# Sixty-four tokens of a product-key expert layer leave the dense grid for gathered rows on VectorE

## The chip, the cores and the metric

The kernel runs as one program on one core of one Trainium2 chip. The metric is the time of one execution in microseconds of device time. Engines are named as in the profile: PE is TensorE (PEld its weight loads), DVE is VectorE, ACT is ScalarE, POOL is GpSimd, SP the queue that issues most DMAs. Each engine runs its instructions in its own fixed order; an instruction waits until its inputs are there and its buffer is free, and all that is behind it on its engine waits with it.

## The reference

One layer of a decoder for 256 tokens of width 2048, float32: a mixer (sliding-window attention and an mLSTM, gated and merged), and then a channel mixer that looks experts up. The change touches only the second.

```python
qp = (xt @ w_peer_q).reshape(T, 8, 2, 128)
scores = einsum('thcd,hcnd->thcn', qp, peer_keys)        # 128 keys in each half
s_top, i_top = top_k(scores, 16)
cand = s_top[:, :, 0, :, None] + s_top[:, :, 1, None, :]
top_s, pos = top_k(cand.reshape(T, 8, 256), 16)
idx = take_along_axis(cand_idx, pos)                     # 16 of 16384 experts per head
gates = softmax(top_s)
act = gelu(einsum('td,thkd->thk', xt, peer_u[idx]))
x = x + einsum('thk,thkd->td', gates * act, peer_v[idx])
```

So each token has 8 x 16 = 128 experts of its own among 16384; each expert has one row of u and one of v, 2048 numbers (8 KB) each.

## The kernel before

All 256 tokens are worked against all 16384 experts. The experts lie in 128 blocks of 128. In the stage **u** TensorE makes, for each block, the products of 128 experts with 256 tokens; ScalarE takes the Gelu of them into a big table W (parts wA and wB, experts on the partitions, tokens along a row). The 128 gates of a token are *scattered* into that table: a one-hot matrix A (first index) and B (second index) are built for four tokens at a time and multiplied on TensorE (line 853), and the product with the table leaves zero everywhere but at the token's own experts. In the stage **v** TensorE multiplies the table with all of v into eight banks of PSUM that stay open through the stage.

Matmuls run in the type float32r, and each float32 operand is split into a rounded part `hi` (a ScalarE copy, line 84) and the rest `lo` (a VectorE subtraction, line 85). A product is made of three parts: hi·hi, hi·lo and lo·hi.

All weights stream in *units* of 128x1024 (512 KB): `load` has four buffers (raw), hi and lo have two each. Function `run` walks through a list of units; for each it issues the load and the split of the next unit, then the matmuls of the present one, and then as many entries of a list of small tasks (`side`: the top-16 searches, the lookups, the scatters) as the rate in its call allows. A u unit is half a block (`ws_units`): eight 512-column matmuls (line 158: X holds the hi and lo of 256 tokens side by side) and eight of 256 columns (line 162). A v unit has twelve 512-column matmuls (lines 889 to 893), with the table's column as the weights.

The work is written as such a program order, and the instructions of each engine are then put into a fixed order by the framework's scheduler, which moves an instruction forward where it thinks that its engine would be free. So the order on an engine isn't always that of the code. The rates in the code are hints to it.

Stages after the mixer: w_o with the residual x1, the query projection (w_pq, 32 units, with `score` and `top16`), u in two calls of `run` (52 blocks with the rest of the searches, `pick16`, `lookup` and `turn`; then 76 blocks with the scatters), v, and the output. The tile X (64 KB a partition) holds the tokens' operand and later the residual.

Of the kernel before, what the change touches and what calls it, by code (L numbers as in the profile page):

```python
# [29 lines left out]
LOW = -3.0e38  # L30
HU = 1024
QU = 512


@with_exitstack
def hybrid_block_kernel(ctx: ExitStack, tc: tile.TileContext, a, out):
# [10 lines left out]
    def pool(stack, name, bufs=1):  # L47
        return stack.enter_context(tc.tile_pool(name=name, bufs=bufs, reuse_waits="tile"))
# [34 lines left out]
    def split(hi, lo, src):  # L83
        S.activation(hi, src, AF.Copy)  # L84
        V.tensor_sub(lo, src, hi.bitcast(F32))  # L85
# [45 lines left out]

# [704 lines left out]
    W[1] = wpool.tile([P, NE - NA, T], F32, name="wB")  # L836
    TG = 4
    NAB = 8

    def scatter(t0):  # L840

        AB = []
        for j in range(TG):
            t = t0 + j
            AB.append(eb.tile([P, 2, NK], F32, name="ab", bufs=NAB))
            A, B = AB[j][:, 0], AB[j][:, 1]
            S.activation(B, iot, AF.Square, bias=i1T[:, t:t + 1])  # L847
            S.activation(B, B, AF.Relu, bias=1.0, scale=-1.0)
            V.tensor_scalar(A, iot, i0T[:, t:t + 1], gT[:, t:t + 1], op0=OP.is_equal, op1=OP.mult)  # L849
        yield  # L850
        ps = psd.tile([P, TG, NK], F32, name="sd")
        for j in range(TG):
            PE.matmul(ps[:, j], AB[j][:, 1], AB[j][:, 0], start=True, stop=True)  # L853
        yield
        m = done["e"]
        for s, (lo, hi) in enumerate(((0, NA), (NA, NE))):
            for x0, x1, mul in ((lo, min(max(m, lo), hi), True), (max(min(m, hi), lo), hi, False)):
                if x1 <= x0:
                    continue
                dst = W[s][:, x0 - lo:x1 - lo, t0:t0 + TG].rearrange("p i t -> p t i")  # L860
# [4 lines left out]
        done["tok"] = t0 + TG  # L865
# [6 lines left out]
    acc = [[(psd, pmm)[t].tile([P, QU], F32, name=("sd", "mm")[t]) for q in range(4)] for t in range(NT)]  # L872
    pw = {}
    x1 = xx.tile([P, NT, D], F32, name="X")
    nc.sync.dma_start(x1, x1d.rearrange("(t p) d -> p t d", p=P))

    def v_consume(i, h):
        def f(parts):
            if h == 0:
                ph = eb.tile([P, T], F32R, name="ph", tag="ab", bufs=NAB)  # L880
                pl = eb.tile([P, T], F32R, name="pl", tag="ab", bufs=NAB)
                split(ph, pl, wv(i))
                pw[i] = (ph, pl)
            ph, pl = pw[i]
            hi, lo = [[part[:, q * QU:(q + 1) * QU] for q in range(HU // QU)] for part in parts]
            todo = [(q, t) for q in range(HU // QU) for t in range(NT)]
            for q, t in todo:
                ts = slice(t * P, (t + 1) * P)
                PE.matmul(acc[t][h * 2 + q], ph[:, ts], hi[q], start=(i == 0), stop=False)  # L889
                PE.matmul(acc[t][h * 2 + q], pl[:, ts], hi[q], start=False, stop=False)  # L890
            for q, t in todo:
                ts = slice(t * P, (t + 1) * P)
                PE.matmul(acc[t][h * 2 + q], ph[:, ts], lo[q], start=False, stop=(i == NE - 1))  # L893
        return f

    units = []
    for i in range(NE):
        for h in range(2):
            units.append((a["v"][i * P:(i + 1) * P, h * HU:(h + 1) * HU], v_consume(i, h)))
    run(units)  # L900
    for q in range(4):
        for t in range(NT):
            o = x1[:, t, q * QU:(q + 1) * QU]
            V.tensor_add(o, acc[t][q], o)
            nc.sync.dma_start(out[t * P:(t + 1) * P, q * QU:(q + 1) * QU], o)


# [59 lines left out]
```

## Time and profile before

| | |
|---|---|
| time, median of 3 runs | 2269.59 us (2269.19 to 2269.6) |
| the profiled execution | 2268.72 us, span of the trace 2267.0 us |
| busy in the span | PE 99%, PEld 84%, DVE 71%, ACT 55%, POOL 4% |
| moved | 415.66 MB, 183 GB/s on average |
| TensorE's granted clock | full (0.999 on average) |

The span runs from the first instruction to the last; the execution's time has a little around it. A matmul's recorded length reaches from its issue to its modelled end and overlaps the next one's, so its price is the distance between starts. The profile's stretches used below, in us from the start of the span: 684 to 778 the query projection, 778 to 1067 the first 52 blocks of u, 1067 to 1556 the other 76, 1556 to 2262 v.

### The profile page before, as it was taken

The page shows a single profiled execution, that of the slowest core. Times are in us where ns is not written, and L with a number is a line of the kernel's source. Part 1 is how long each engine was busy: PE and PEld are TensorE (multiplying, and loading weights), DVE is VectorE, ACT ScalarE, POOL GpSimd, SP SyncE. Part 2 cuts the span into 40 slices and gives each one's busy share as a digit, 9 for nine tenths or more (in the row PEclk, how much of TensorE's full clock was granted, in tenths as well). Part 3 has the DMA queues.
Part 4 walks back from the last instruction along what each step waited for, and adds up shares of the span by engine and source line. Part 5 has one row for each costly group of instructions (what it writes and reads, how often), then busy time and mean ns, then how long its engine had stood idle before and what let it go on. Part 6 is the DMA issues. An engine that isn't in the chain of part 4 may idle for free.

```text
span 2267.0 us, 32407 instructions
## 1 busy us (share of the span) xinstructions
PE 2235.2 (99%) x11841; PEld 1906.3 (84%) x11841; DVE 1599.0 (71%) x2915; ACT 1257.8 (55%) x2378; POOL 85.9 (4%) x79
## 2 busy tenths in 40 slices
PE   7999999999999999999999999999999999999999
PEld 5887788888888878888888888888888888888887
DVE  7977688778889997855777788886555555555555
ACT  5755566556544444544777777775444444444443
POOL 3000000000130020200000000000000000000000
PEclk9999999999999999999999999999999999999999
DMA  6565544555665445555544444556555555555555
GB/s 204 189 191 164 169 160 160 184 186 189 211 212 188 162 164 196 181 190 186 171 165 166 165 163 167 165 170 213 195 195 193 193 194 193 194 194 193 194 192 173
DMA packets 115296, 415.66 MB, mean 183 GB/s; under 512 B 12992, under 2 KB 13120, under 8 KB 114752
## 3 DMA queue, kind: packets, MB, share of 16 engines
q1 hardware_dynamic: 115136, 413.59, 55.1%
q8 instruction: 92, 1.51, 0.3%
q14 instruction: 68, 0.56, 0.1%
HBM read 409.35 MB, written 4.19 MB: 182 GB/s over the span
## 4 chain that ended last, share of the span: by engine, by line
PE 91%; DVE 7%; ACT 1%; POOL 1%; issue 0%; DMA 0%; POOLq 0%; SPq 0%; DVEq 0%
PE mm L158 33%; PE mm L162 17%; PE sd L890 5%; PE sd L889 5%; PE mm L889 5%; PE mm L890 5%; PE sd L893 5%; PE mm L893 5%; PE sd L853 3%; DVE lo L85 2%; PE mm L184 2%; PE mm L185 2%; PE mm L189 2%; DVE oh L805 0%; DVE xg L257 0%
## 5 line engine op out<-in xcount | busy, mean ns | idle before, releaser
L85 DVE TENSOR_TENSOR lo<-raw,hi 128x1024 fp32r<-128x1024 f32 x762 | 936.5, 1229 | 611.3 <-ACT hi L84 603.4
L84 ACT ACTIVATE hi<-raw 128x1024 fp32r<-128x1024 f32 x762 | 807.0, 1059 | 863.1 <-PE mm L890 378.5
L158 PE MATMUL mm<-X,hi 128*128 128x512 f32 x3088 | 789.8, 397 | 13.8 <-ACT hi L84 8.5
L158 PEld LDWEIGHTS mm<-X,hi 128*128 128x128 f32 x3088 | 557.4, 190 | 117.7 <-ACT hi L84 8.8
L162 PEld LDWEIGHTS mm<-X,lo 128*128 128x128 f32 x3088 | 421.1, 190 | 39.7 <-DVE lo L85 9.7
L162 PE MATMUL mm<-X,lo 128*128 128x256 f32 x3088 | 433.6, 283 | 5.0 <-DVE lo L85 5.0
L889 PE MATMUL sd<-hi,ph 128*128 128x512 f32 x512 | 199.2, 389 | 0.0
L890 PE MATMUL sd<-hi,pl 128*128 128x512 f32 x512 | 199.2, 389 | 0.0
L890 PE MATMUL mm<-hi,pl 128*128 128x512 f32 x512 | 199.2, 389 | 0.0
L889 PE MATMUL mm<-hi,ph 128*128 128x512 f32 x512 | 199.2, 389 | 0.0
L893 PE MATMUL sd<-lo,ph 128*128 128x512 f32 x512 | 199.2, 389 | 0.0
L893 PE MATMUL mm<-lo,ph 128*128 128x512 f32 x512 | 199.2, 389 | 0.0
L889 PEld LDWEIGHTS mm<-hi,ph 128*128 128x128 f32 x512 | 96.1, 188 | 20.1
L893 PEld LDWEIGHTS sd<-lo,ph 128*128 128x128 f32 x512 | 96.1, 188 | 20.0
L890 PEld LDWEIGHTS mm<-hi,pl 128*128 128x128 f32 x512 | 96.1, 188 | 19.9
L889 PEld LDWEIGHTS sd<-hi,ph 128*128 128x128 f32 x512 | 96.1, 188 | 19.9
L893 PEld LDWEIGHTS mm<-lo,ph 128*128 128x128 f32 x512 | 96.1, 188 | 19.9
L890 PEld LDWEIGHTS sd<-hi,pl 128*128 128x128 f32 x512 | 96.0, 188 | 19.9
L184 PE MATMUL mm<-hi,X 128*128 128x512 f32 x224 | 89.6, 400 | 0.0
L847 ACT ACTIVATE ab<-iot,i1T 128x128 f32<-128x128 f32 x256 | 87.8, 390 | 1.4 <-DVE i1T L823 1.4
L185 PE MATMUL mm<-hi,X 128*128 128x512 f32 x224 | 88.2, 394 | 0.0
L849 DVE TENSOR_SCALAR ab<-iot,i0T,gT 128x128 f32<-128x128 f32 x256 | 74.2, 345 | 0.0
(279 smaller groups left out, 2082.4 us busy)
## 6 DMA issues: line engine op xcount, KB each, us to landing
raw<-u SPq DMA_DIRECT2D x256, 512.0 KB, 3.7
raw<-v SPq DMA_DIRECT2D x256, 512.0 KB, 3.6
raw<-w_g SPq DMA_DIRECT2D x64, 512.0 KB, 3.6
raw<-w_tok SPq DMA_DIRECT2D x56, 512.0 KB, 3.6
raw<-w_qk SPq DMA_DIRECT2D x32, 512.0 KB, 3.7
raw<-w_o SPq DMA_DIRECT2D x32, 512.0 KB, 4.0
raw<-w_pq SPq DMA_DIRECT2D x32, 512.0 KB, 3.7
raw<-w_pa SPq DMA_DIRECT2D x16, 512.0 KB, 3.5
```

Of the source, the lines that this page charges most:

```text
L84: S.activation(hi, src, AF.Copy)
L85: V.tensor_sub(lo, src, hi.bitcast(F32))
L158: PE.matmul(ps, hi[:, w], X[:, k].rearrange("p s t -> p (s t)"), start=(k == 0), stop=False)
L162: PE.matmul(ps[:, :T], lo[:, w], X[:, k, 0], start=False, stop=(k == kts - 1))
L184: PE.matmul(st["ps"][t], xh[:, k, ts], hi[q], start=(k == 0), stop=False)
L185: PE.matmul(st["ps"][t], xl[:, k, ts], hi[q], start=False, stop=False)
L847: S.activation(B, iot, AF.Square, bias=i1T[:, t:t + 1])
L849: V.tensor_scalar(A, iot, i0T[:, t:t + 1], gT[:, t:t + 1], op0=OP.is_equal, op1=OP.mult)
L853: PE.matmul(ps[:, j], AB[j][:, 1], AB[j][:, 0], start=True, stop=True)
L889: PE.matmul(acc[t][h * 2 + q], ph[:, ts], hi[q], start=(i == 0), stop=False)
L890: PE.matmul(acc[t][h * 2 + q], pl[:, ts], hi[q], start=False, stop=False)
L893: PE.matmul(acc[t][h * 2 + q], ph[:, ts], lo[q], start=False, stop=(i == NE - 1))
```

## The change

Tokens 0 to 63 leave the table. For them the rows of their own experts are gathered from memory: `fetch` is an indirect DMA on POOL's queue that brings 128 half rows of 1024 numbers (4 KB), one to a partition: partitions 0 to 63 hold the first half of the row for the 64 tokens, 64 to 127 the second. One fetch serves one of the 128 expert slots, so there are 128 fetches from u and 128 from v, 512 KB each, into six slabs in the place of the tile X. `dot` multiplies a slab with the tokens and sums along the row on VectorE; `own_weights` adds the two halves on TensorE, takes the Gelu and the gate; `add_row` adds a v row times its weight into `xs_`.

The other 192 tokens (ND) stay on TensorE, now already scaled with the norm: `xg` is written to memory while w_o runs, read back and split into Xn. A u unit has 24 matmuls of 192 columns, three for each weight block of 128x128, and ends in PSUM without a sum or scaling by VectorE; a v unit has 24 as well, with the blocks of v as the weights and the table's column (in the ring in Xn's place) moving, so that the output comes out transposed and is turned back in `finish`. The scatter runs for 192 tokens, with the one-hot A for four tokens in one VectorE instruction and the gate moved into ScalarE's Relu. The second token tile's top-16 searches are put behind the first's lookups.

```diff
+SP = 64
+ND = T - SP
+HD = D // 2
@@ step
+        if rows_todo:
+            pace[1] += row_rate[0]
+            if pace[1] >= 1.0:
+                pace[1] -= 1.0
+                rows_todo.pop(0)()
@@ evac_out
+            S.dma_start(xgd[:, n], xg[:, SP:])
@@
-    NA = 80
-    wA = exc.tile([P, NA, T], F32, name="wA")
+    Xn = exc.tile([P, KT, 2, ND], F32R, name="Xn")
+    NA = 74
+    wA = exc.tile([P, NA, ND], F32, name="wA")
+    def load_xg():
+        nc.sync.dma_start(wA[:, 0:KT], xgd)
+    def norm_xg(c):
+        xs = wA[:, 4 * c:4 * c + 4]
+        V.tensor_mul(xs, xs, rb[:, SP:].unsqueeze(1).to_broadcast([P, 4, ND]))
+        split(Xn[:, 4 * c:4 * c + 4, 0], Xn[:, 4 * c:4 * c + 4, 1], xs)
+    side += [load_xg] + [lambda c=c: norm_xg(c) for c in range(KT // 4)]
@@ u_units
-            z = eb.tile([P, T], F32, name="zu")
-            total(z, ps)
-            V.tensor_mul(z, z, rb)
-            later.append(lambda: act_u(i, z))
+                for j in range(per):
+                    k = h * per + j
+                    w = slice(j * P, (j + 1) * P)
+                    PE.matmul(o, hi[:, w], Xn[:, k, 0], start=(k == 0), stop=False)
+                    PE.matmul(o, hi[:, w], Xn[:, k, 1], start=False, stop=False)
+                for j in range(per):
+                    k = h * per + j
+                    w = slice(j * P, (j + 1) * P)
+                    PE.matmul(o, lo[:, w], Xn[:, k, 0], start=False, stop=(k == KT - 1))
+                if h == KT // per - 1:
+                    later.append(lambda: act_u(i, ps))
-    E0 = 52
+    E0 = 44
@@ the rows of tokens 0 to 63
+    sp = xx.tile([P, 2 * KT * T], F32, name="X")
+    NSL = 6
+    slab = [sp[:, j * HD:(j + 1) * HD] for j in range(NSL)]
+    def fetch(table, s):
+        G.indirect_dma_start(out=slab[s % NSL], out_offset=None, in_=tables[table],
+                             in_offset=bass.IndirectOffsetOnAxis(ap=ix[:, s:s + 1], axis=0))
+    def own_rows():
+        V.tensor_scalar(ixf, ixf, 2.0, half, op0=OP.mult, op1=OP.add)
+        V.tensor_copy(ix, ixf)
+        for s in range(NSL):
+            fetch("u", s)
+        rows_todo.extend([lambda s=s: dot(s) for s in range(NS)])
+    def dot(s):
+        V.scalar_tensor_tensor(slab[s % NSL], slab[s % NSL], 1.0, xs_, op0=OP.mult, op1=OP.mult,
+                               accum_out=dots[:, s:s + 1])
+        if s + NSL < NS:
+            fetch("u", s + NSL)
+    def add_row(s):
...
+            V.scalar_tensor_tensor(xs_, slab[s % NSL], wgt[:, s:s + 1], xs_, op0=OP.mult, op1=OP.add)
+        if s + NSL < NS:
+            fetch("v", s + NSL)
@@ calls
-    run(u_units(0, E0), 0.75)
+        if t == 0:
+            side += [own_index, lambda: None, lambda: None, lambda: None, own_rows]
+    own_x()
+    row_rate[0] = 0.7
+    run(u_units(0, E0), 1.0)
@@ scatter
+        V.tensor_tensor(A, iot.unsqueeze(1).to_broadcast([P, TG, NK]),
+                        i0T[:, t0:t0 + TG].unsqueeze(2).to_broadcast([P, TG, NK]), op=OP.is_equal)
-    side += [scatter(t0) for t0 in range(0, T, TG)]
+    side += [scatter(t0) for t0 in range(SP, T, TG)]
@@ v
-                PE.matmul(acc[t][h * 2 + q], ph[:, ts], hi[q], start=(i == 0), stop=False)
-                PE.matmul(acc[t][h * 2 + q], pl[:, ts], hi[q], start=False, stop=False)
+            for o, b, w in blocks:
+                PE.matmul(o, hi[:, w], ph, start=False, stop=False)
+                PE.matmul(o, hi[:, w], pl, start=False, stop=False)
+            for o, b, w in blocks:
+                PE.matmul(o, lo[:, w], ph, start=False, stop=(i == NE - 1 and b % 2 == 1))
+    rows_todo += [lambda s=s: add_row(s) for s in range(NS)]
+    row_rate[0] = (NS + 1) / (len(units) - 2 * LAST - 2)
```

The engines' orders, first VectorE's in the u stage. Line 85 before and line 88 now is the lo split of a unit; 199 and 769 are the sum and scaling of a u block, 805 and 808 a lookup. Before, in the first part of u:

```order
L85 TENSOR_TENSOR lo<-raw,hi 128x1024
L199 TENSOR_TENSOR zu<-mm,zu 128x256
L808 TENSOR_REDUCE iv<-oh 128x16
L769 TENSOR_TENSOR zu<-zu,rb 128x256
L808 TENSOR_REDUCE iv<-oh 128x16 x2
L85 TENSOR_TENSOR lo<-raw,hi 128x1024
```

And now, from the tenth unit of u on (912 is a dot, 848 the lookup's first instruction):

```order
L844 CAST abf<-ab 128x256
L912 SCALAR_TENSOR_TENSOR X<-X 128x1024
L848 TENSOR_TENSOR oh<-abf,a_7748 128x256 x2
L912 SCALAR_TENSOR_TENSOR X<-X 128x1024
L848 TENSOR_TENSOR oh<-abf,a_7748 128x256
L912 SCALAR_TENSOR_TENSOR X<-X 128x1024 x2
L88 TENSOR_TENSOR lo<-raw,hi 128x1024
L912 SCALAR_TENSOR_TENSOR X<-X 128x1024 x6
L88 TENSOR_TENSOR lo<-raw,hi 128x1024
```

The sum and scaling are gone. All 128 dots stand between the sixth lo split of u and the thirty-third, five or six in most of these 27 gaps; after the last of them some forty gaps hold a lo split and nothing else. The code's rate was 0.7 dots a unit.

VectorE in the v stage: `pl` before and the split into Xn now is the split of the table's column, 936 the weighted add of a row. Before, all through v:

```order
L85 TENSOR_TENSOR pl<-wA,ph 128x256
L85 TENSOR_TENSOR lo<-raw,hi 128x1024 x2
L85 TENSOR_TENSOR pl<-wA,ph 128x256
L85 TENSOR_TENSOR lo<-raw,hi 128x1024 x2
L85 TENSOR_TENSOR pl<-wA,ph 128x256
```

Now, from the sixth unit of v on:

```order
L936 SCALAR_TENSOR_TENSOR X<-X 128x1024 x6
L88 TENSOR_TENSOR lo<-raw,hi 128x1024
L88 TENSOR_TENSOR Xn<-wA,Xn 128x192
L936 SCALAR_TENSOR_TENSOR X<-X 128x1024 x5
L88 TENSOR_TENSOR lo<-raw,hi 128x1024
L936 SCALAR_TENSOR_TENSOR X<-X 128x1024 x5
```

The 128 adds stand in the first 25 gaps of v, up to the twenty-sixth lo split, though the code spreads them over 242 units.

TensorE at the change from the query projection to u. Before (730 is `score`):

```order
L162 MATMUL mm<-X,lo 128x256 x6
L730 MATMUL sd<-keysT,zu 128x128 x2
L162 MATMUL mm<-X,lo 128x256 x2
L158 MATMUL mm<-X,hi 128x512 x8
L162 MATMUL mm<-X,lo 128x256 x8
```

Now, at the end of u's first unit (the pair of 811 and 812 stands eight times before the eight of 816):

```order
L811 MATMUL mm<-Xn,hi 128x192
L812 MATMUL mm<-Xn,hi 128x192
L816 MATMUL mm<-Xn,lo 128x192 x8
L811 MATMUL mm<-Xn,hi 128x192
L812 MATMUL mm<-Xn,hi 128x192
```

A unit had 16 matmuls and has 24, of 192 columns each; the scatters and transposes keep their places between units.

## Rows read from the trace of the kernel before

**Rows 1.** The page: engines' busy time and share; the chain that ended last.
```profile
PE 2235.2 (99%) x11841; PEld 1906.3 (84%) x11841; DVE 1599.0 (71%) x2915; ACT 1257.8 (55%) x2378; POOL 85.9 (4%) x79
...
PE 91%; DVE 7%; ACT 1%; POOL 1%; issue 0%; DMA 0%; POOLq 0%; SPq 0%; DVEq 0%
```

**Rows 2.** Windows: stretch, length, busy PE PEld DVE ACT POOL, clock, DMA share, GB/s.
```profile
684.00:778.00 94.00, 92.14 (x527) 79.12 (x528) 89.36 (x339) 41.48 (x61) 0.00 (x0) 1.00 0.50 171
778.00:1067.00 289.00, 283.47 (x1614) 245.81 (x1613) 218.15 (x420) 146.12 (x223) 36.51 (x32) 1.00 0.55 182
1067.00:1556.00 489.00, 489.00 (x2985) 436.62 (x2984) 381.66 (x738) 357.03 (x969) 0.00 (x0) 1.00 0.50 167
1556.00:2262.00 706.00, 705.59 (x3128) 584.48 (x3126) 364.15 (x396) 313.00 (x387) 0.00 (x0) 1.00 0.59 194
```

**Rows 3.** Timeline of TensorE in a scatter unit: start, length (us), line.
```profile
1199.73 1.12 PE L162 MATMUL mm<-X,lo 128*128 128x256 f32 x8
1200.68 1.06 PE L853 MATMUL sd<-ab 128*128 128x128 f32 x8
```

**Rows 4.** Windows, a stretch of v.
```profile
1700.00:1800.00 100.00, 100.00 (x443) 82.81 (x442) 50.75 (x56) 45.05 (x56) 0.00 (x0) 1.00 0.58 192
```

**Rows 5.** Groups by shape: busy us, mean ns, idle; 128-column passes, loads of weights.
```profile
L853 PE MATMUL sd<-ab 128*128 128x128 f32 x512 | 66.3, 275 | 0.0
...
L853 PEld LDWEIGHTS sd<-ab 128*128 128x128 f32 x512 | 62.1, 192 | 0.0
...
L518 PEld LDWEIGHTS sd<-pT,av 128*64 128x64 f32 x48 | 2.4, 134 | 3.9 <-issue 3.7 <-ACT hi L84 0.2
```

**Rows 6.** Timeline of TensorE, plain f32 matmuls of 257 columns, two passes each.
```profile
332.07 0.59 PE L574 MATMUL sd<-v,dT 128*128 128x257 f32 x2
332.50 0.60 PE L575 MATMUL sd<-v,dT 128*128 128x257 f32 x2
```

**Rows 7.** Groups by shape, VectorE.
```profile
L85 DVE TENSOR_TENSOR lo<-raw,hi 128x1024 fp32r<-128x1024 f32 x762 | 936.5, 1229 | 611.3 <-ACT hi L84 603.4 <-PE sd L853 4.5 <-ACT sr L78 0.6
...
L85 DVE TENSOR_TENSOR pl<-wA,ph 128x256 fp32r<-128x256 f32 x80 | 33.4, 419 | 0.2 <-ACT ph L84 0.2
...
L85 DVE TENSOR_TENSOR X<-xg,X 128x256 fp32r<-128x256 f32 x32 | 23.8, 765 | 0.6 <-ACT X L84 0.6
...
L356 DVE SCALAR_TENSOR_TENSOR ac<-zqk,acol,ac 128x256 f32<-128x256 f32 x48 | 23.2, 483 | 0.6
...
L805 DVE TENSOR_TENSOR oh<-abf,a 128x256 f32<-128x256 f32 x32 | 14.2, 481 | 0.0
...
L808 DVE TENSOR_REDUCE iv<-oh 128x16 f32<-128x256 f32 x32 | 12.7, 411 | 4.9 <-POOL oh L807 4.9
```

**Rows 8.** DMA queue (page), start of the kernel (windows), landing of loads (DMA issues).
```profile
q1 hardware_dynamic: 115136, 413.59, 55.1%
...
10.00:15.00 5.00, 1.90 (x5) 1.54 (x6) 5.00 (x14) 3.08 (x7) 3.11 (x5) 1.00 1.03 416
...
raw<-u SPq DMA_DIRECT2D x256, 512.0 KB, 3.7
```

**Rows 9.** Groups by shape, GpSimd.
```profile
L807 POOL TENSOR_TENSOR oh<-oh,itf 128x256 f32<-128x256 f32 x32 | 36.5, 1159 | 224.1 <-DVE gs L815 119.2 <-DVE oh L805 104.9
...
L684 POOL TENSOR_TENSOR sqa<-sqa,sq 128x256 f32<-128x256 f32 x15 | 26.5, 1767 | 60.7 <-ACT sq L680 60.7
...
L249 POOL TENSOR_TENSOR sq<-xt 128x256 f32<-128x256 f32 x5 | 3.2, 643 | 0.1
```

**Rows 10.** Groups by shape, ScalarE.
```profile
L84 ACT ACTIVATE hi<-raw 128x1024 fp32r<-128x1024 f32 x762 | 807.0, 1059 | 863.1 <-PE mm L890 378.5 <-PE mm L158 277.4 <-issue 126.9
...
L847 ACT ACTIVATE ab<-iot,i1T 128x128 f32<-128x128 f32 x256 | 87.8, 390 | 1.4 <-DVE i1T L823 1.4
...
L848 ACT ACTIVATE ab<-ab 128x128 f32<-128x128 f32 x256 | 64.5, 299 | 0.1
```

**Rows 11.** Timelines of TensorE and VectorE at the end.
```profile
2261.20 0.39 PE L893 MATMUL mm<-lo,ph 128*128 128x512 f32 x1
...
2262.75 0.68 DVE L904 TENSOR_TENSOR X<-mm,X 128x512 f32<-128x512 f32 x1
```

More of the change, by code (lines that the diff above doesn't have):

```diff
@@ L97, in parts_of @@
         return hi, lo
-    side, later = [], []
-    pace = [0.0]
+    side, later, rows_todo = [], [], []
+    pace = [0.0, 0.0]
+    row_rate = [0.0]
     def tick():
@@ L732, in score @@
         for t in range(NT):
-            side.append(lambda t=t: top16(sc[:, t, n], st_[:, t, n], it_[:, t, n]))
+            (side, second)[t].append(lambda t=t: top16(sc[:, t, n], st_[:, t, n], it_[:, t, n]))
     def evac_q(n):
@@ L745, in hybrid_block_kernel @@
         units += ws_units(a["w_pq"][n], X2, evac_q(n))
-    run(units, 0.75)
+    run(units, 0.85)
     flush()
@@ L824, in turn @@
         V.tensor_copy(gT[:, t * P:(t + 1) * P], pi[:, 2 * P:3 * P])
+        V.tensor_scalar(ngT[:, t * P:(t + 1) * P], pi[:, 2 * P:3 * P], -1.0, None, op0=OP.mult)
+    sp = xx.tile([P, 2 * KT * T], F32, name="X")
+    NSL = 6
+    slab = [sp[:, j * HD:(j + 1) * HD] for j in range(NSL)]
+    xs_ = sp[:, NSL * HD:(NSL + 1) * HD]
+    s0 = (NSL + 1) * HD
+    ixf, dots, wgt, wt = (sp[:, s0 + j * NS:s0 + (j + 1) * NS] for j in range(4))
+    ix = sp[:, s0 + 4 * NS:s0 + 5 * NS].bitcast(U32)
+    zt = sp[:, s0 + 5 * NS:s0 + 5 * NS + SP]
@@ new lines, in own_index @@
+    def own_index():
+        V.tensor_mul(xs_, xs_, slab[NSL - 1])
+        ef = tk.tile([SP, NS], F32, name="ef")
+        V.scalar_tensor_tensor(ef, iv[0:SP, 0], float(NK), iv[0:SP, 1], op0=OP.mult, op1=OP.add)
+        G.dma_start(exd, ef)
+        for c in range(2):
+            G.dma_start(ixf[c * SP:(c + 1) * SP], exd)
+    def own_rows():
[4 more added lines that the diff above has]
+        rows_todo.extend([lambda s=s: dot(s) for s in range(NS)])
@@ new lines, in dot, with own_weights @@
+    def dot(s):
[3 more added lines that the diff above has]
+            fetch("u", s + NSL)
+    def own_weights():
+        for s in range(NSL):
+            fetch("v", s)
+        zp = psd.tile([P, QU], F32, name="sd")
+        PE.matmul(zp[:, 0:SP], dots, pair, start=True, stop=True)
+        yield
+        V.tensor_mul(zt, zp[:, 0:SP], rb[:, 0:SP])
+        S.activation(zt, zt, AF.Gelu)
+        V.tensor_mul(wt.rearrange("p (c t) -> p c t", c=2), zt.unsqueeze(1).to_broadcast([P, 2, SP]),
+                     gT[:, 0:SP].unsqueeze(1).to_broadcast([P, 2, SP]))
+        yield
+        wp = psd.tile([P, QU], F32, name="sd")
+        PE.transpose(wp[:, 0:NS], wt, ident)
+        V.tensor_copy(wgt, wp[:, 0:NS])
@@ L864, in scatter @@
                     S.activation(dst, ps[:, :, x0:x1], AF.Copy)
-        done["tok"] = t0 + TG
-    side += [scatter(t0) for t0 in range(0, T, TG)]
+        done["tok"] = c0 + TG
+    side += [scatter(t0) for t0 in range(SP, T, TG)]
     run(u_units(E0, NE), 3 * len(side) / (2 * (NE - E0) - 5))
     drain()
[L872 to L875, printed above, removed]
+    while rows_todo:
+        rows_todo.pop(0)()
@@ new lines, in hybrid_block_kernel, with load_x1 @@
+    NB2 = D // P
+    acc = [(psd, pmm)[q % 2].tile([P, QU], F32, name=("sd", "mm")[q % 2]) for q in range(NB2 // 2)]
+    NR = 16
+    ring = exc.tile([P, NR, 2, ND], F32R, name="Xn")
+    zero = ring[:, NR - 1].rearrange("p s t -> p (s t)")
+    V.memset(zero.bitcast(F32), 0.0)
+    flat = wA.rearrange("p i t -> p (i t)")
+    x1 = flat[:, 0:2 * D].rearrange("p (t d) -> p t d", d=D)
+    x1s = flat[:, 2 * D:2 * D + HD]
+    def load_x1():
+        nc.sync.dma_start(x1[0:P - SP, 0], x1d[SP:P])
+        nc.sync.dma_start(x1[:, 1], x1d[P:T])
+        for c in range(2):
+            nc.sync.dma_start(x1s[c * SP:(c + 1) * SP], x1d[0:SP, c * HD:(c + 1) * HD])
@@ L877, in v_consume @@
     def v_consume(i, h):
         def f(parts):
+            ph, pl = ring[:, i % NR, 0], ring[:, i % NR, 1]
             if h == 0:
-                ph = eb.tile([P, T], F32R, name="ph", tag="ab", bufs=NAB)
-                pl = eb.tile([P, T], F32R, name="pl", tag="ab", bufs=NAB)
                 split(ph, pl, wv(i))
[L883 to L886, printed above, removed]
@@ L900, in hybrid_block_kernel @@
-    run(units)
[L901 to L905, printed above, removed]
+            hi, lo = parts
+            blocks = [(acc[b // 2][:, (b % 2) * ND:(b % 2 + 1) * ND], b, slice(j * P, (j + 1) * P))
+                      for j, b in enumerate(range(h * (NB2 // 2), (h + 1) * (NB2 // 2)))]
+            if i == 0:
+                for o, b, w in blocks[::2]:
+                    PE.matmul(acc[b // 2][:, 0:2 * ND], hi[:, w], zero, start=True, stop=False)
@@ new lines, in f, with unit, finish @@
+            for o, b, w in blocks:
[3 more added lines that the diff above has]
+                PE.matmul(o, lo[:, w], ph, start=False, stop=(i == NE - 1 and b % 2 == 1))
+        return f
+    def unit(i, h):
+        return (a["v"][i * P:(i + 1) * P, h * HU:(h + 1) * HU], v_consume(i, h))
+    def finish(q):
+        tT = slab[q][:, 0:4 * ND].rearrange("p (b t) -> p b t", t=ND)
+        S.activation(tT[:, 0:2], acc[2 * q][:, 0:2 * ND].rearrange("p (b t) -> p b t", t=ND), AF.Copy)
+        V.tensor_copy(tT[:, 2:4], acc[2 * q + 1][:, 0:2 * ND].rearrange("p (b t) -> p b t", t=ND))
+        for t in range(NT):
+            n = P - SP if t == 0 else P
+            pt = (psd, pmm)[t].tile([P, QU], F32, name=("sd", "mm")[t])
+            for b in range(4):
+                src = tT[:, b, 0:n] if t == 0 else tT[:, b, P - SP:]
+                PE.transpose(pt[0:n, b * P:(b + 1) * P], src, ident)
+            o = x1[0:n, t, q * QU:(q + 1) * QU]
+            V.tensor_add(o, pt[0:n], o)
+            nc.sync.dma_start(out[SP:P, q * QU:(q + 1) * QU] if t == 0 else out[P:T, q * QU:(q + 1) * QU], o)
@@ new lines, in own_out @@
+    def own_out():
+        V.tensor_add(xs_, xs_, x1s)
+        for c in range(2):
+            nc.sync.dma_start(out[0:SP, c * HD:(c + 1) * HD], xs_[c * SP:(c + 1) * SP])
+    LAST = 6
+    units = [unit(i, h) for i in range(NE - LAST) for h in range(2)]
+    units += [unit(i, h) for h in range(2) for i in range(NE - LAST, NE)]
+    ow = own_weights()
+    next(ow), next(ow), next(ow, None)
+    rows_todo += [lambda s=s: add_row(s) for s in range(NS)]
+    rows_todo.append(own_out)
+    row_rate[0] = (NS + 1) / (len(units) - 2 * LAST - 2)
@@ L908, with at_end, f, with_x1 @@
+    pace[1] = 0.0
+    def at_end(u):
+        def f(parts):
+            u[1](parts)
+            later.extend([lambda: finish(0), lambda: finish(1)])
+        return (u[0], f)
+    units[-LAST - 1] = at_end(units[-LAST - 1])
+    x0 = units[100]
+    def with_x1(parts):
+        x0[1](parts)
+        load_x1()
+    units[100] = (x0[0], with_x1)
+    run(units)
+    flush()
+    while rows_todo:
+        rows_todo.pop(0)()
+    finish(2)
+    finish(3)
 def kernel(**inputs):
```

78 lines of the change are left out of this document (48 added, 30 removed).

## The prediction

> **What bounds the kernel now.** I read the chain that ended last first: TensorE is 91% of it [rows 1]. Then busy time by stage [rows 2]. The four stretches are the query projection of the retrieval (684 to 778 us), the first 52 blocks of u (to 1067), the other 76 with the scatter of the gates beside them (to 1556), and v. TensorE's clock is granted in full in all of them (the 2.4 GHz level), and TensorE is busy for all but 8 us of 1578. VectorE is at 95%, 75%, 78% and 52% of its time in them, ScalarE at 44 to 73%, the DMA engines at 50 to 59%. So TensorE sets the pace, and what counts is the time from one matmul to the next, not its recorded length (matmuls overlap). The eight 256-column matmuls of a u unit take 1200.68 - 1199.73 = 0.95 us, 0.119 each [rows 3]. The 512-column ones of v: 443 in 100 us, 0.226 each [rows 4]. The eight 128-column passes of a scatter take 1.06 us in all, the last 0.275 by its own record, so (1.06 - 0.275)/7 = 0.112 each [rows 3, 5].
>
> **TensorE's part of the change.** A 128x128 block of u costs one 512-column and one 256-column matmul, 0.345 us; v costs 24 matmuls of 0.226 per expert block. The new code has three matmuls of 192 columns for a weight block in both stages, each with its own weight load, as every matmul of the trace has one [rows 1]: 2048 x 3 x 2 = 12288 matmuls, against 4096 + 3072. No row has a matmul of this type under 256 columns. From below: if the time went with the columns, 0.226 x 192/512 = 0.085. From above, two prices: 0.119, if 192 columns cost what 256 do; and 0.321, if the type lost its rate, since plain f32 passes of 257 columns stand 0.43 apart per two passes [rows 6], 1.67 ns a column. I take 0.112, the nearest row in length and the one with the same weight load: 0.192 us recorded for 128 columns of weights, 0.134 for 64 [rows 5], that is 0.9 ns a column and 0.116 for 128, so a weight load alone seems to fill what a 192-column stream leaves free. The Trainium skill (TensorE: Matmul & The Clock Gate, "LDWEIGHTS (loading the stationary operand)") says that a load lasts its columns divided by 1.2 ns, 107 ns here, whatever streams beside it. That rule speaks against this change, and by it the final sum would come to 2559 us.
>
> At 0.112: 12288 x 0.112 = 1376 us against 2048 x 0.345 + 3072 x 0.226 = 707 + 694 = 1401: 25 saved. Only 48 of 64 scatter groups stay, 16 x 8 x 0.112 = 14 saved. The eight zeroing matmuls add 1. **Sum -38 us**: three narrow matmuls are hardly cheaper than two wide ones. A unit (half a block) then takes 24 x 0.112 = 2.69 us.
>
> **VectorE's part, which decides.** What VectorE loses (the 0.42 us sum and scaling of each u block) lay beside TensorE: worth nothing. What it gains is 128 dots and 128 weighted adds on 128x1024. The nearest rows are the same operation on 256 elements, 0.483 us, and two-input work of 256 and 1024 elements, 0.419 and 1.229 [rows 7]: 0.483 + 0.810 = 1.29 us each, 165 us a stage. Spread evenly over the stages that would fit. But the order of VectorE's instructions doesn't spread them: in u all 128 dots stand in 27 gaps between one lo split and the next (from the sixth unit on, five or six to a gap), in v all 128 adds in 25 gaps. VectorE works in that order, and TensorE can run only two units ahead of the last lo (two buffers of hi and lo).
>
> In those 27 gaps of u VectorE has 165 + 27 x 1.23 = 198, and 21 of picks and lookups for the second token tile [rows 7]: 219 us, where TensorE needs 27 x 2.69 = 73. In the 25 gaps of v: 165 + 31 + 10 for 29 splits of the gates (0.35 each), 206 us against 67.
>
> The rows must arrive too: 128 gathers of 0.524 MB plus the stage's own loads, 155 x 0.524 = 81 MB in u and 80 + 2 in v. The DMA queue moved 413.59 MB in 55.1% of 2267 us [rows 8], 331 GB/s at full share, which makes 246 us; at the 416 GB/s of the start [rows 8] it is 195. So VectorE and the DMA engines need about the same time, six gathers are in flight, and they won't mesh perfectly: I take 240 us for u, 235 for v. What issuing a gather costs on GpSimd no row shows: from below nothing (hidden), from above the whole 3.7 us landing of a 512 KB load [rows 8] for one gather after another, 474 us a stage. The nearest row, GpSimd's work on 128x256, is 1.16 us [rows 9]; that is under the 1.29 of a dot, so I price it at nothing beyond the 240.
>
> TensorE's stalls: u **240 - 73 = +167**; v **235 - 67 = +168**.
>
> Smaller terms. In the four gaps before the dots, VectorE has 29 us (sixteen lookups of 0.481 + 0.411 among them), GpSimd's 16 x 1.16 in one go adds 4, and the expert numbers' way through DRAM (two landings, less 4 of other work) 2: 35 - 4 x 2.69 = 24, of which the run-up hides little: **+23**. In the query projection the reload, scaling and split of xg put 10.2 us into one gap; the others have about 2.4 against 2.77: **+5** (0 to 12). A scatter group's four Squares and four Relus (4 x 0.689, [rows 10]) stand in one ScalarE gap between hi splits, often with the next group's in the gap after it: about 8 us with the splits (1.06 each) and a Gelu, against 5.4. There are 24 such pairs; TensorE's scatter passes and hi's head start of half a unit hide most: **+10** (0 to 60). At the start of v the gate splits reuse the place of Xn and must wait for u's last matmul, then the weights of the rows go matmul, product, Gelu, product, transpose, copy: **+6** (3 to 12). At the end two last transposed quarters replace four adds; now 5.8 us lie between the last matmul's start and the end of the span [rows 11]: **+4**. The early place of the row output among SP's loads (after 30 of 256) costs nothing, since VectorE finishes those adds at the same place.
>
> **Sum**, on the profiled execution's 2268.7 us (span 2267.0; 0.9 under the median): 2268.7 - 38 + 5 + 23 + 167 + 10 + 6 + 168 + 4 = 2614. The saving on TensorE is real and small; two stretches in which everything waits for gathered rows cost nine times as much. Behind them what is late next is TensorE again, at 2.69 us a unit.
>
> **Rivals.**
> (a) *Gather and dot hold each other up.* GpSimd's adds took 1.77 us beside a busy VectorE, its products 0.64 in a calmer place [rows 9], and VectorE's split of X beside those adds 0.765 on average, against 0.419 for the same shape elsewhere [rows 7]: +0.35, up to 0.55 in the worst. If a gather costs GpSimd 1.77 and lengthens a dot by 0.55, one after the other, a gather's period is 2.3: 128 x 2.3 + 33 = 327 in u, 335 in v. That adds 87 + 100: 2801 us. Against it: six slabs let issue and dot overlap. The Trainium skill (SBUF — State Buffer, "Who interferes with whom") says that a VectorE instruction with two SBUF inputs contends with a GpSimd instruction that reads SBUF; the split's row agrees, and dots and adds have two such inputs.
> (b) *The narrow matmul loses its rate*: 0.321 us. For it: plain f32 does run so [rows 6]. Against it: one weight load and one pass stand for each such matmul, as for the wide ones. Then 12288 x (0.321 - 0.112) = 2568 more, a unit of 7.7 us covers the row work (the three stalls go, -358): 4824 us.
> (c) *Faster, the other side: the time goes with the columns*, weight loads hidden. For it: from 256 to 512 columns the price rises by 0.107, nearly in proportion. Against it: 128-column passes cost 0.112. The stalls stay, since VectorE sets them, and TensorE's cheaper units make them longer. With the gathers hidden too (219 and 206) the total is 1328 + 11040 x price (12288 matmuls, less 52 x 24 inside the two stretches): at 0.085, 2266 us, no slower than before. It decides at 0.0852 us.
> (d) *The row work doesn't stall anything*, because VectorE's idle time (25% and 48% of u and v) takes it: 2614 - 358 = 2256. Only with the dots spread over the stage; the order has them in 27 and 25 gaps.
>
> **How the numbers follow.** Forecast 62%, (a) 18%, (b) 10%, (c) 3%, (d) 2%; 5% for something slower that I haven't named. The likeliest case's own range is 2490 to 2710: low with VectorE alone as the limit (219, 206: -50), no ScalarE or projection loss (-15) and the matmul at 0.107 (11040 x 0.005 = -55); high with 0.119 (+77) and more of ScalarE's clumps. To hold 8 in 10 the range must take in (a); the upper bound of gathers one after another is 2614 + 234 + 239 = 3087. I give 2470 to 3000. (b), (c) and (d) are left out, with 15%, and a little at either end. About 0.2% (4.5 us) is what a measurement can tell from no change: (d) and half of (c) make faster 3%, the other half and a little of (d) same 2%, and the rest slower, 95%.
>
> **What would show it.** In u's first 33 units and v's first 26 TensorE should be busy a third of its time, VectorE near full, DMA share over 0.9, and the span of each stretch near 240 us. The dots should last 1.29. Outside them matmuls should start 0.112 apart and a unit take 2.7 us, TensorE full. If VectorE shows idle time before the dots and ends it on a DMA, and GpSimd's issue is longer than 1.3 us, (a) holds. If matmuls of 192 columns stand 0.3 us apart, (b). I am wrong altogether if VectorE's trace has the dots spread over the stage, or lo splits passing them.

## The result: 2599 us against 2269

The changed kernel took 2599.23 us (median of 4 runs, 2595.2 to 2601.38), the kernel before 2269.39 (4 runs): a ratio of 1.1452, 95% interval 1.1432 to 1.1472. Forecast were 2614, in 2470 to 3000. The profiled execution has a span of 2598.9 us, 331.9 longer.

### The profile page after: what moved, and what is told of

It reads as the page before. It is cut to its first block, busy times and chain, and to the rows that moved or that the text cites. A ratio compares the mean times of both kernels' runs of the same rounds, so it can differ in the third digit from the quotient of the medians.

```text
span 2598.9 us, 42839 instructions
## 1 busy us (share of the span) xinstructions
PE 2335.0 (90%) x16876; PEld 2200.9 (85%) x16876; DVE 1771.0 (68%) x2843; ACT 1205.0 (46%) x2113; POOL 421.1 (16%) x343
## 5 line engine op out<-in xcount | busy, mean ns | idle before, releaser
L811 PE MATMUL mm<-Xn,hi 128*128 128x192 f32 x2048 | 516.7, 291 | 6.8 <-ACT hi L87 6.3
L812 PE MATMUL mm<-Xn,hi 128*128 128x192 f32 x2048 | 511.2, 289 | 0.0
L811 PEld LDWEIGHTS mm<-Xn,hi 128*128 128x128 f32 x2048 | 425.0, 208 | 9.8 <-ACT hi L87 9.8
L812 PEld LDWEIGHTS mm<-Xn,hi 128*128 128x128 f32 x2048 | 424.6, 207 | 0.0
L816 PE MATMUL mm<-Xn,lo 128*128 128x192 f32 x2048 | 300.3, 293 | 131.3 <-DVE lo L88 131.3
L816 PEld LDWEIGHTS mm<-Xn,lo 128*128 128x128 f32 x2048 | 274.4, 208 | 138.1 <-DVE lo L88 138.1
L1025 PE MATMUL sd<-Xn,lo 128*128 128x192 f32 x1024 | 212.6, 290 | 90.1 <-DVE lo L88 90.1
L167 PE MATMUL mm<-X,hi 128*128 128x512 f32 x1040 | 271.8, 402 | 15.3 <-ACT hi L87 8.1
L1022 PE MATMUL sd<-Xn,hi 128*128 128x192 f32 x1024 | 270.5, 288 | 0.0
L1022 PE MATMUL mm<-Xn,hi 128*128 128x192 f32 x1024 | 268.9, 287 | 0.0
L1023 PE MATMUL sd<-Xn,hi 128*128 128x192 f32 x1024 | 268.8, 286 | 0.0
L1023 PE MATMUL mm<-Xn,hi 128*128 128x192 f32 x1024 | 267.5, 285 | 0.0
L1025 PEld LDWEIGHTS sd<-Xn,lo 128*128 128x128 f32 x1024 | 166.8, 205 | 95.5 <-DVE lo L88 95.5
L167 PEld LDWEIGHTS mm<-X,hi 128*128 128x128 f32 x1040 | 190.0, 191 | 53.6 <-DVE X L88 9.5
L1022 PEld LDWEIGHTS sd<-Xn,hi 128*128 128x128 f32 x1024 | 210.5, 206 | 0.0
L1023 PEld LDWEIGHTS sd<-Xn,hi 128*128 128x128 f32 x1024 | 210.2, 205 | 0.0
L1025 PE MATMUL mm<-Xn,lo 128*128 128x192 f32 x1024 | 209.9, 289 | 0.0
L1022 PEld LDWEIGHTS mm<-Xn,hi 128*128 128x128 f32 x1024 | 209.1, 204 | 0.0
L1023 PEld LDWEIGHTS mm<-Xn,hi 128*128 128x128 f32 x1024 | 209.0, 204 | 0.0
```

Of the source, the lines that this page charges most:

```text
L167: PE.matmul(ps, hi[:, w], X[:, k].rearrange("p s t -> p (s t)"), start=(k == 0), stop=False)
L811: PE.matmul(o, hi[:, w], Xn[:, k, 0], start=(k == 0), stop=False)
L812: PE.matmul(o, hi[:, w], Xn[:, k, 1], start=False, stop=False)
L816: PE.matmul(o, lo[:, w], Xn[:, k, 0], start=False, stop=(k == KT - 1))
L1022: PE.matmul(o, hi[:, w], ph, start=False, stop=False)
L1023: PE.matmul(o, hi[:, w], pl, start=False, stop=False)
```

## The profile after

Engines over the span, as in [rows 1]:

```profile
PE 2335.0 (90%) x16876; PEld 2200.9 (85%) x16876; DVE 1771.0 (68%) x2843; ACT 1205.0 (46%) x2113; POOL 421.1 (16%) x343
```

TensorE has 100 us more than before and VectorE 172, in a span that is 332 longer. Nothing is full on average, so the stages must be read. Windows of before, cut at the starts of VectorE's lo splits, the last one at TensorE's end (columns as in [rows 2]): the query projection, the four gaps before the dots, the 27 gaps, the rest of u, the first 25 gaps of v, its other 230 units:

```profile
676.40:784.70 108.30, 104.94 (x600) 89.94 (x599) 102.73 (x374) 47.26 (x70) 3.63 (x4) 1.00 0.52 178
784.70:796.30 11.60, 11.31 (x67) 9.88 (x66) 11.53 (x39) 6.87 (x9) 0.00 (x0) 1.00 0.49 151
796.30:876.40 80.10, 76.61 (x432) 64.95 (x431) 77.21 (x176) 39.11 (x56) 20.71 (x19) 1.00 0.51 173
876.40:1565.50 689.10, 687.58 (x4120) 610.48 (x4119) 509.81 (x927) 459.52 (x1130) 15.80 (x13) 1.00 0.52 173
1565.50:1633.50 68.00, 68.00 (x301) 56.29 (x301) 35.65 (x41) 30.68 (x39) 0.00 (x0) 1.00 0.66 224
1633.50:2261.60 628.10, 628.09 (x2771) 519.74 (x2770) 322.64 (x348) 277.19 (x341) 0.00 (x0) 1.00 0.58 191
```

The same units of the changed kernel:

```profile
676.20:790.80 114.60, 106.77 (x601) 91.84 (x599) 107.82 (x370) 50.43 (x74) 4.24 (x6) 0.97 0.53 183
790.80:833.40 42.60, 22.37 (x133) 21.54 (x132) 40.62 (x129) 7.71 (x10) 17.67 (x26) 0.66 0.30 85
833.40:1089.40 256.00, 141.14 (x648) 135.20 (x649) 211.72 (x370) 41.56 (x60) 194.18 (x144) 0.57 0.88 319
1089.40:1745.60 656.20, 650.51 (x5755) 647.46 (x5755) 358.45 (x440) 403.31 (x851) 6.65 (x5) 0.99 0.54 185
1745.60:1970.30 224.70, 135.57 (x649) 130.01 (x648) 199.17 (x185) 36.05 (x55) 153.25 (x122) 0.59 0.96 354
1970.30:2593.30 623.00, 621.66 (x5536) 621.19 (x5536) 314.35 (x342) 268.67 (x331) 0.00 (x0) 0.99 0.58 194
```

Lengths, after less before: +6.3, +31.0, +175.9, -32.9, +156.7, -5.1. They make the 331.9. In the third and the fifth row VectorE is busy for 83% and 89% of the time, the DMA engines for 0.88 and 0.96; no single engine is full, yet TensorE does 27 units in 256 us. What the waits of VectorE and GpSimd (us in total, times, longest) come to in u's 27 gaps:

```profile
DVE X L912 <- DMA X<-ur,X: 40.9, 30, 3.3
...
POOL X L883 <- issue: 33.8, 112, 0.3
POOL X L883 <- DVE X L912: 20.7, 13, 5.3
```

VectorE waits 40.9 us for rows (22.3 in v's 25 gaps). GpSimd is busy for 194 us and spends 34 more between one gather and the next (about 0.30 each time) without a wait that the profile shows: 228 of 256, nearer to full than VectorE, as far as spans on GpSimd can be read. One gap of that stretch shows how TensorE is held up. VectorE's timeline (start, length, line; in brackets the idle time and its releaser):

```profile
952.28 1.22 DVE L912 SCALAR_TENSOR_TENSOR X<-X 128x1024 f32<-128x1024 f32 x1
953.42 0.09 DVE L912 DVE_READ_ACCUMULATOR X<-X 128x1 f32 x1
956.14 1.22 DVE L912 SCALAR_TENSOR_TENSOR X<-X 128x1024 f32<-128x1024 f32 x1 [2.63 <-DMA X<-ur,X]
957.29 0.08 DVE L912 DVE_READ_ACCUMULATOR X<-X 128x1 f32 x1
957.29 1.22 DVE L88 TENSOR_TENSOR lo<-raw,hi 128x1024 fp32r<-128x1024 f32 x1
```

and TensorE's beside it:

```profile
953.78 0.41 PE L811 MATMUL mm<-Xn,hi 128*128 128x192 f32 x1
954.00 0.41 PE L812 MATMUL mm<-Xn,hi 128*128 128x192 f32 x1
958.56 2.02 PE L816 MATMUL mm<-Xn,lo 128*128 128x192 f32 x8 [4.15 <-DVE lo L88]
```

A dot waits 2.63 us for its row; the lo split stands behind it on VectorE; TensorE, done with hi, waits 4.15 us for that lo. The matmuls there start 0.21 us apart: the granted clock is 0.57 in this stretch, 0.59 in that of v, where TensorE waits in nearly every unit, so for most of it the clock stands at the lower of its two levels (1.2 GHz). A unit of 24 then takes 5.1 us, still under the 9.5 and 9.0 us that the gaps last, so the clock isn't what sets the gaps. In a full stretch of v they stand 0.11 apart:

```profile
2150.85 0.27 PE L1022 MATMUL sd<-Xn,hi 128*128 128x192 f32 x1
2150.96 0.27 PE L1023 MATMUL sd<-Xn,hi 128*128 128x192 f32 x1
2151.07 0.28 PE L1022 MATMUL sd<-Xn,hi 128*128 128x192 f32 x1
2151.18 0.27 PE L1023 MATMUL sd<-Xn,hi 128*128 128x192 f32 x1
```

Over all neighbours of this kind the median is 0.113 (2044 pairs), and full units of u and v start 2.68 us apart (median).

## Experiments

Seven kernels were run. The stretches in the expectations are cut otherwise (845 to 1090.5 and 1745.6 to 1971.5 us: 245.6 and 225.9) than in the windows here (256.0 and 224.7): in u both ends lie one gap later, in v the second.

**1. The row work tied to the code's units.**

```diff
-    def dot(s):
-        V.scalar_tensor_tensor(slab[s % NSL], slab[s % NSL], 1.0, xs_, op0=OP.mult, op1=OP.mult,
+    def dot(s, lo):
+        V.tensor_scalar(tied[:, s:s + 1], lo[:, 0:1].bitcast(F32), 0.0, 1.0, op0=OP.mult, op1=OP.add)
+        V.scalar_tensor_tensor(slab[s % NSL], slab[s % NSL], tied[:, s:s + 1], xs_, op0=OP.mult, op1=OP.mult,
...
```

`lo` is that of the unit in which the code puts the dot. (`add_row` likewise, with 0 times lo plus the weight.)

> Each dot and each weighted add reads a scalar that VectorE makes, in one tiny instruction, from a lo unit of the step in which the code puts it, so that VectorE's order has at most one dot or add in a gap between lo splits (in u from unit 30 on). Matmuls, gathers and bytes are unchanged; 256 tiny instructions are added. Theory (the two stretches cost 320 us because 128 dots and 128 adds stand in 27 and 25 gaps): both stretches go, less some 12 us for a lump of lookups of the second token tile: 2599 - 165 - 155 + 12 = 2290 us (2270 to 2330), granted clock full again. Rival (row work costs TensorE its price wherever it stands, through the DMA engines' share or VectorE's port): the stalls stay in small pieces, over 2450 us.

Measured: 2285.91 us, ratio to before 1.0074 (1.0057 to 1.0091), so still 0.7% behind it. The 27 gaps, the rest of u, and the 25 gaps of v:

```profile
834.60:930.40 95.80, 81.18 (x615) 80.20 (x616) 63.71 (x120) 39.16 (x58) 19.54 (x21) 0.86 0.55 181
930.40:1587.40 657.00, 650.74 (x5788) 647.58 (x5788) 526.64 (x816) 405.10 (x853) 198.46 (x127) 1.00 0.81 283
1587.40:1656.70 69.30, 69.01 (x613) 68.84 (x613) 54.90 (x83) 33.48 (x53) 24.91 (x13) 1.00 0.87 300
```

The same gathers, dots, adds and matmuls, in another order on VectorE and with 256 tiny instructions more, are 313 us shorter. The rest of u now carries nearly all the dots and is no longer than it was without them (657.0, 656.2). The rival falls.

**2. Without the gathers.**

```diff
-        V.scalar_tensor_tensor(slab[s % NSL], slab[s % NSL], 1.0, xs_, op0=OP.mult, op1=OP.mult,
+        V.scalar_tensor_tensor(slab[NSL - 1], slab[s % (NSL - 1)], 1.0, xs_, op0=OP.mult, op1=OP.mult,
...
-        if s + NSL < NS:
-            fetch("u", s + NSL)
...
-        if s + NSL < NS:
-            fetch("v", s + NSL)
```

> Only the first six gathers of each stage are made; dots and adds read those slabs again and again (so the rows are the wrong ones), and a dot's product goes to one slab. VectorE keeps the order: five or six dots or adds to a gap. Theory (VectorE's work is the floor of both stretches, its waits for gathered rows, 41 and 25 us, lie on top): u's stretch 245.6 to about 205, v's 225.9 to about 201, in all 2533 us (2515 to 2550). Rival (the gathers set the pace, and lengthen dots and loads too): a dot falls well under 1.2 us, the stretches under 180, in all under 2490.

Measured: 2537.24 us (one run).

```profile
831.00:1051.70 220.70, 133.94 (x627) 128.24 (x627) 213.01 (x370) 40.07 (x58) 24.41 (x24) 0.60 0.24 81
1708.40:1909.90 201.50, 132.23 (x643) 127.11 (x643) 198.21 (x185) 36.08 (x55) 0.00 (x0) 0.63 0.25 78
```

VectorE alone, 97% and 98% busy, needs 221 and 202 us, for which the prediction had 219 and 206. In the expectation's cut u's stretch is 214 us, where I expected 205: dots in a row start 1.26 us apart in this run, against 1.14 in the changed kernel, so a part of the 221 comes with the edit. A dot lasts 1.226 us instead of 1.235: the gathers hardly lengthen it.

**3. Gathers with short dots.**

```diff
-        V.scalar_tensor_tensor(slab[s % NSL], slab[s % NSL], 1.0, xs_, op0=OP.mult, op1=OP.mult,
+        V.scalar_tensor_tensor(slab[s % NSL][:, 0:32], slab[s % NSL][:, 0:32], 1.0, xs_[:, 0:32], op0=OP.mult, op1=OP.mult,
...
```

(`add_row` likewise.)

> All 256 gathers are made, but each dot and add takes 32 of the 1024 numbers of a slab (the rest of the row is left out); the order still has five to a gap, in 25 and 25 gaps. Theory (VectorE and the gathers need nearly the same time): the stretches hardly shrink, since the gathers bind next, at 1.26 to 1.40 us of GpSimd each (161 to 179 us) or 82 MB at the 350 GB/s of now (234 us): 195 to 225 us each, in all 2510 to 2580, 2545 taken. Rival (VectorE's arithmetic alone makes the stalls and the gathers hide): stretches near 75 to 95 us, in all near 2300.

Measured: 2537.42 us (one run).

```profile
832.00:1048.10 216.10, 134.25 (x627) 128.61 (x627) 82.79 (x370) 39.95 (x58) 148.27 (x145) 0.60 0.97 376
1702.60:1910.30 207.70, 131.82 (x649) 126.73 (x648) 68.68 (x186) 36.07 (x55) 128.95 (x122) 0.63 1.00 384
```

With VectorE at 38% and 33% of its time the stretches still last 216 and 208 us: now the DMA engines are full, and GpSimd isn't (148 of 216). So VectorE's work and the transfers each need about 210 us, and together, six slabs deep, 256 and 225: neither hides the other wholly. What keeps them from it was not separated: no run has more slabs, and GpSimd's part of a gather, 1.05 us here, lasts 1.40 in the changed kernel's u.

**4. 384 columns for hi in u.**

```diff
-                    PE.matmul(o, hi[:, w], Xn[:, k, 0], start=(k == 0), stop=False)
-                    PE.matmul(o, hi[:, w], Xn[:, k, 1], start=False, stop=False)
+                    PE.matmul(ps[:, :2 * ND], hi[:, w], Xn[:, k].rearrange("p s t -> p (s t)"), start=(k == 0), stop=False)
...
+                    z = eb.tile([P, ND], F32, name="zn")
+                    S.activation(z, ps[:, ND:2 * ND], AF.Copy)
+                    V.tensor_add(z, ps[:, :ND], z)
```

> In u alone, hi times Xn's two halves is one matmul of 384 columns instead of two of 192; the halves are summed by a ScalarE copy and a VectorE add per block, as before the change. This moves VectorE's order too: the dots now stand two or three to a gap in some 60 gaps; v is unchanged. Theory (192 columns cost 0.113 because of the weight load, 384 cost 0.226 x 384/512 = 0.170): a calm u unit falls from 2.72 to 8 x (0.170 + 0.113) = 2.27 us; u's first part is VectorE's at about 4.6 us a unit over 60 units, so u takes about 790 us instead of 955, in all 2434 (2400 to 2480). Rival (a matmul costs its columns, at any width): two of 192 cost what one of 384 does, a calm unit stays 2.72, in all over 2520.

Measured: 2451.54 us, ratio 1.0804 (1.0786 to 1.0822). The two halves of a calm unit, by TensorE's timeline:

```profile
1399.80 1.03 PE L815 MATMUL mm<-Xn,lo 128*128 128x192 f32 x8
1400.67 1.59 PE L811 MATMUL mm<-Xn,hi 128*128 128x384 f32 x8
1402.10 1.03 PE L815 MATMUL mm<-Xn,lo 128*128 128x192 f32 x8
```

Eight of 192 take 0.87 us and eight of 384 1.43, that is 0.109 and 0.179 each (medians 0.112 and 0.175), 2.30 us a unit. One of 384 is cheaper than two of 192 by 0.05, so the price doesn't go by columns below 256. A floor of about 0.11 us binds a narrow matmul; that the weight load sets it is argued, not shown. In all it is 17 us over what was expected. In the second part of the dots' stretch and a little beyond, the DMA share is 0.99 and VectorE at 88%; whether the transfers make the 17 us is not shown, since VectorE waits only 12 us for rows there.

```profile
942.60:1147.30 204.70, 149.96 (x822) 137.26 (x822) 180.90 (x276) 68.21 (x103) 136.65 (x97) 0.86 0.99 384
```

The edit moves VectorE's order too, and the 148 us gained on the changed kernel have both causes. The same 185 units of u, from its 73rd lo split on, in the changed kernel and here:

```profile
1197.20:1745.60 548.40, 543.00 (x4828) 540.18 (x4828) 309.56 (x398) 357.73 (x793) 0.00 (x0) 1.00 0.53 179
1119.90:1593.00 473.10, 469.39 (x3337) 466.38 (x3337) 337.81 (x493) 384.97 (x885) 1.68 (x1) 1.00 0.65 210
```

These 75 us go with the wide matmul, for no dots stand there. Before them u is 77 us shorter (329.9 against 406.4), with two or three dots to a gap instead of five or six; the two causes are mixed there.

**5. Both edits.** (The edits of 1 and 4 together.)

> Both edits: dots and adds tied to the code's units, and 384-column matmuls for hi in u. Theory (with the row work spread, TensorE and VectorE each set u's pace in turn: units of 8 x (0.175 + 0.113) = 2.30 us with the scatters' 43 us make 632, VectorE's own work in u 672 and 128 tiny instructions of 0.15): u near 730 us against 795 in the tied kernel; v as there: 2286 - 65 = 2221 us (2195 to 2245), below the kernel before. Rival (the sum over two halves per block, 0.35 us of VectorE more, brings the stalls back): u over 780, in all 2270 or more.

Measured: 2225.17 us, ratio 0.9799 (0.9783 to 0.9815): 2.0% faster than before, as expected.

**6. Both edits, 0.6 dots a unit, lo widened.**

```diff
-                    PE.matmul(o, lo[:, w], Xn[:, k, 0], start=False, stop=(k == KT - 1))
+                    PE.matmul(ps[:, :T], lo[:, w], Xn[:, k].rearrange("p s t -> p (s t)")[:, :T], start=False, stop=(k == KT - 1))
...
-    row_rate[0] = 0.7
+    row_rate[0] = 0.6
```

> As the one with both edits, with 0.6 dots a unit instead of 0.7, so that they reach to u's end, and with lo's matmul widened from 192 to 256 columns (it then adds the product lo x Xn's lo part for 64 tokens, a term of the true product that was left out). The wider lo moves VectorE's order: the lookups of both token tiles stand in small pieces, at most 5.5 us in a gap, instead of lumps. Theory (what is left of stalls in u is lumps in VectorE's order; TensorE pays 2048 x 0.006 = 12 us more): u near 715, in all 2206 us (2180 to 2235). Rival (TensorE's pace decides in u by now): 12 us slower than the kernel with both edits alone.

Measured: 2179.19 us, ratio 0.9605 (0.9589 to 0.9621), the best of all, 27 us under the expected 2206 and just outside its range; the rival, 12 us slower than experiment 5, falls. The four gaps, the 27, and the rest of u:

```profile
789.10:802.60 13.50, 10.70 (x72) 10.05 (x71) 11.01 (x35) 6.60 (x9) 1.73 (x4) 1.00 0.80 204
802.60:876.30 73.70, 67.35 (x435) 64.26 (x435) 68.54 (x158) 43.24 (x73) 29.46 (x26) 0.98 0.70 237
876.30:1476.70 600.40, 582.11 (x3982) 567.13 (x3983) 569.63 (x1000) 441.97 (x968) 238.20 (x144) 0.99 0.88 310
```

u takes 687.6 us where I expected 715. The lumps of lookups are gone (13.5 us in the four gaps, against 42.5 in experiment 1). TensorE is 97% busy in the rest of u, VectorE 95%, the DMA share is 0.88. Which of the two edits gave more, the rate or the wider lo, was not separated.

**7. No row work.**

```diff
-        G.indirect_dma_start(out=slab[s % NSL], out_offset=None, in_=tables[table],
-                             in_offset=bass.IndirectOffsetOnAxis(ap=ix[:, s:s + 1], axis=0))
+        pass
...
-        rows_todo.extend([lambda s=s: dot(s) for s in range(NS)])
+        V.memset(dots, 0.0)
...
-    rows_todo += [lambda s=s: add_row(s) for s in range(NS)]
```

> The change without its row work: no gathers, no dots, no adds (the experts' part of tokens 0 to 63 is left out); the rest as changed. Theory (the row work cost its two stretches, and spread it costs nothing): what the tied kernel took, 2286 less a few: 2270 to 2290, 2281 taken, that is, the dense part alone is no faster than the 256 tokens before, because narrow matmuls save 31 us and VectorE's lump of lookups at u's start gives 37 back. Rival (spread row work still costs TensorE through DMA or VectorE): under 2260.

Measured: 2281.51 us (one run), within 5 us of the tied kernel, which does all of the row work. The four gaps at u's start are as long as with the rows:

```profile
788.50:831.10 42.60, 23.36 (x132) 22.84 (x132) 40.71 (x129) 7.71 (x10) 15.24 (x23) 0.72 0.27 81
926.80:1582.40 655.60, 650.13 (x5789) 647.46 (x5788) 359.59 (x440) 404.44 (x853) 0.00 (x0) 1.00 0.56 182
```

So the kernel with 192 tokens on TensorE is no faster than that with 256: the rest of u and v are 38 us shorter (narrow matmuls, 16 scatter groups fewer, and stalls of before that are gone), and 51 go into the lumps of lookups at u's start (31 in the four gaps, 15.6 in the 27) and the projection (4).

## Why the prediction was right, step by step

- **The matmul's price** (0.112 taken): 0.113, and 2.68 us a unit (2.69). Rivals (b) and (c) fall with it. The 107 ns that the Trainium skill gives for a load (TensorE: Matmul & The Clock Gate, "LDWEIGHTS (loading the stationary operand)") is 5% under it; the nearly equal prices of 128, 192 and 256 columns (0.112, 0.113, 0.119) agree with the rule's form. No run shows the 0.107 of the range's low end.
- **The stretch of u** (240 us): 256.0. VectorE alone 221 (219 taken), the transfers alone 216 (195 to 246). The term for imperfect meshing was too small, 21 taken over VectorE's 219, 35 found; in the changed kernel itself VectorE waits 41 us for rows, and its own work is 215.
- **The stretch of v** (235 us): 224.7; VectorE alone 202 (206), the transfers 208. Here the meshing term was too large, 29 taken, 23 found.
- **A dot** (1.29 us): recorded at 1.235 with 0.082 for reading the sum, but dots in a row start 1.14 apart; an add lasts 1.287. The sum of 219 came out near by two errors: by the distances between starts, waits left out, dots and the reading of their sums take 152 us in u's stretch (165 taken), and what stands there beside them and the lo splits 28 (21 taken).
- **A gather's issue on GpSimd** (nothing, as shorter than a dot): in u 1.40 us and 0.30 to the next, 1.70 together, longer than a dot; in v 1.26 and 0.30. So the reason for pricing it at nothing failed, and whether it has a part in the 35 to 41 us is open.
- **Before the dots** (35 us in four gaps): 42.6, and 42.6 without any row work. There the first instruction of a lookup took 0.751 us against 0.481 in [rows 7], with GpSimd's products beside it; sixteen of them at 0.27 more explain 4 of the 7.6.
- **The query projection** (+5): +6.3.
- **ScalarE's scatter clumps (+10), v's start (+6), the tail (+4)**: hardly there. In the rest of u TensorE waits 4.3 us for hi splits; 225 units at 2.69 us and 43 for 48 scatter groups make 648 of its 656.2. v's first gaps hold no more than VectorE's work and rows. From the start of the last product's matmul to the end it is 7.8 us, before 5.8.
- **The balance.** Before's windows, with TensorE's saving and these terms, would be 245 us for u's 27 gaps, 34 for the four and 113 for the projection: 11, 8 and 1 too few. They would be 670 for the rest of u, 241 for v's first gaps and 627 for the rest of v: 13, 17 and 4 too many, from the terms above and from some 15 us of stalls that the kernel before had there (its rest of u took 689.1 us where TensorE's prices make 678, the rest of v 628.1 where they make 624) and that are gone. 20 too few and 34 too many leave the 13 us between 2614 and the profiled 2601: the mechanism held, but that the total came so near is in part luck.
- **Rival (a)**, gather and dot holding each other up, needed 327 and 335 us and a dot of 1.8; there were 256 and 225, and 1.24. By the sign that I gave for it, idle time of VectorE that a DMA ends and an issue over 1.3 us, it would hold in u (40.9 us, 1.40 us); so that sign was too weak, and a part of (a) may sit in the meshing term. GpSimd's part of a gather does get longer beside VectorE (1.05 us with short dots, 1.40 in u, up to 1.71 spread through v). The clash that the Trainium skill describes (SBUF — State Buffer, "Who interferes with whom") is of a VectorE instruction with two SBUF inputs and a GpSimd instruction that reads SBUF; no run here shows whether a gather's issue is held up by that.
- **Rival (d)** has its condition met in experiment 1: 2286 us, 30 over its 2256. It dropped the +23 before the dots together with the row work, but lookups make that term, and they stay (42.5 us in the four gaps); more of them stand in the 27 gaps (95.8 us where TensorE needs 73). The terms that were too high give some 20 back.
- **Signs that I gave wrongly**: TensorE "busy a third of its time" in the stretches. It is 55% and 60%, because at the lower clock the same matmuls stand twice as far apart (0.213 us). The DMA share was to be over 0.9 and is 0.88 in u. Outside the stretches TensorE is full, as said.

## What to carry to other kernels

Work for an idle engine is free only where it stands in that engine's order: count the instructions between two that the bound engine waits for, not the engine's share over a stage. Two engines or queues that each need about the stretch's time, coupled through a few buffers, needed 8 and 16% more together here than the slower of them alone. Before splitting a matmul into narrower ones, price it by its row at that width; here two of 192 columns cost 0.226 us and one of 384 0.175.

## What was not expected

TensorE's granted clock was 0.57 and 0.59 in the stretches where it waited in each unit, its matmuls then 0.21 us apart instead of 0.113, and nearly full in the rest of u (0.99), where it didn't wait. A gather of 128 rows of 4 KB kept GpSimd for 1.05 us beside short dots, 1.26 and 1.40 in the changed kernel's stretches, and 1.53 to 1.72 where dots and adds were spread (experiments 1, 5 and 6); with the loads the DMA engines moved 376 to 384 GB/s at a share of 0.97 to 1.00.
